# Seven products of quarters in a feed-forward input projection, with its features passed through DRAM

## The chip, the cores and the metric

The kernel runs on one core of one Trainium2 chip. A core has five engines that run side by side, each in its own order: TensorE (PE in the profile, with its weight loads shown apart as PEld), VectorE (DVE), ScalarE (ACT), GpSimd (POOL), and SyncE (SP), which here issues all transfers between DRAM and SBUF. Matrix products are summed in PSUM, which has eight banks of 512 fp32 numbers per partition. The metric is the device time of one execution in microseconds (us).

## The reference

Two layers of a decoder trunk, all in fp32, on 1024 prompt tokens and 8 sequences of 8 new tokens (1088 token columns in all). Layer 0 mixes tokens with an RG-LRU, layer 1 with HGRN2; after each mixer comes a feed-forward block, and each of the four sublayers ends in a residual sum and a layer norm:

```python
def causal_dwconv(x, buf, w, b):
    xp = jnp.concatenate([buf.astype(x.dtype), x], axis=1)
    y = sum(xp[:, j:j + L] * w[j] for j in range(width)) + b
    return y, xp[:, xp.shape[1] - (width - 1):]

def conv_ffn(x, buf, w_in, cw, cb, w_out):      # w_in 1024 x 5632, w_out 2816 x 1024
    gate, up = jnp.split(x @ w_in, 2, axis=-1)
    gc, new_buf = causal_dwconv(gate, buf, cw, cb)
    return (jax.nn.gelu(gc) * up) @ w_out, new_buf

for i in range(DEPTH):
    ...
    x = layer_norm(ALPHA * x + mix, ln_g[i, 0], ln_b[i, 0])
    f, fbuf = conv_ffn(x, ffn_conv[i], ffn_w_in[i], ffn_conv_w[i], ffn_conv_b[i], ffn_w_out[i])
    x = layer_norm(ALPHA * x + f, ln_g[i, 1], ln_b[i, 1])
```

## The kernel before

**Products.** TensorE multiplies in fp32r. Every fp32 operand is held as two fp32r parts, a high part `h` (the operand cast) and a low part `l` (operand minus `h`), and a product `a b` is made of three: `ah bh + ah bl + al bh`. Activations lie as features by tokens in `x[P, KT, 2, U]` (8 blocks of 128 features, two parts, 1088 tokens).

**Weights.** `stepf` writes down a list of steps, each with blocks of weights that it needs. `issue_raw` (L106) has SP load the next blocks into two staging tiles `raw`; `convert` (L115) splits a staged block of 128x1024 numbers: ACT casts it into the high part (L131) and the engine in `run["lo"]`, POOL from early on, subtracts (L132). Split blocks live in three tiles `wb` and in extra ones (`wx...`) where a stage has room. `pump` (L139) is called between groups of products and splits one block ahead. `fill` and `flush` take small closures from `pend`, which puts other work between the products.

**Feed-forward** (`ffn`, L781). The 2816 features are 22 blocks of 128. For each block `f` the gate product and the up product are made by `inproj` (L217): three chunks of 384, 384 and 320 tokens, each 8 feature blocks x 3 matmuls into one PSUM bank (`in_chunk`, L204). `g_evac` copies a gate out with ACT; `conv` (L829) makes the causal convolution with three DVE operations over 1104 columns, then GELU on ACT; `u_evac` (L844) multiplies by the up product and splits the result into the two parts of a tile `yf` in SBUF. After every two blocks `out_group` makes their share of the output product: 9 tiles of tokens (128 each, the last with the 64 new tokens) by 2 halves of 512 columns, 6 matmuls each, added to the residual in `z` by DVE (`resid`, L254). The last four blocks go in `out_final` with the layer norm.

**Layer norm** (`ln_pipeline`, L305) runs behind the last products of each tile of tokens: statistics on ACT and DVE, `nrm_b` scales on DVE (L281) and multiplies by the gain on POOL (L283), `nrm_c` adds the bias on DVE (L294). `to_x` (L237) then turns the tile into features with 8 transposes on TensorE, 2 ACT copies and 2 DVE subtractions. The last three tiles are left as fills for the next stage, which starts with `inproj_first` (L225), chunks of 512, 256 and 320 tokens. The sum before the first norm of a layer is made in `mix_out` (L434), in two passes of 9 tiles, one per half of the columns. `z` stays in SBUF between the two norms of a layer.

Of the kernel before, what the change touches and what calls it, by code (L numbers as in the profile page):

```python
# [18 lines left out]
P = 128  # L19
D = 1024  # L20
# [20 lines left out]
CH_FIRST = ((0, 512), (512, 256), (768, 320))  # L41
TW = 1152
# [14 lines left out]
def hawk_hgrn2_convffn_deepnorm_kernel(  # L57
# [15 lines left out]
    x = cp.tile([P, KT, 2, U], FR, name="x")  # L73
# [11 lines left out]
    zsave = dpool.tile([NT * P, D], F32, name="zsave")  # L85
    raws = [cp.tile([P, 1024], F32, name=f"raw{i}", tag=f"raw{i}") for i in range(2)]
# [5 lines left out]
    # ---------------------------------------------------------------- weight stream  # L92
# [4 lines left out]
    wfree = {"b": deque(wbase), "x": deque()}  # L97

    def stepf(phase, descr, fn, pref=None, keep=False):
        ids = []  # L100
        for i, b in enumerate(descr):
            blocks.append([phase, b, None, None, pref[i] if pref else "b"])
            ids.append(len(blocks) - 1)
        steps.append((phase, ids, fn, keep))

    def issue_raw(n=2):  # L106
        while run["dma"] < min(len(blocks), run["cvt"] + n) and rawq:
            b = blocks[run["dma"]]
            raw = rawq.popleft()
            dst, src = b[1](raw)  # L110
            sp.dma_start(dst, src)
            b[2] = raw
            run["dma"] += 1

    def convert():  # L115
        """Splits the next block of weights into its two parts, if a place for it is free."""
# [3 lines left out]
        kind = b[4]  # L120
        here = b[0] == run["phase"]
# [4 lines left out]
        b[4] = kind  # L126
        w = wfree[kind].popleft()
        issue_raw()
        raw = b[2]
        n = b[1].cols  # L130
        act.copy(w[:, 0, :n], raw[:, :n])  # L131
        run["lo"].tensor_tensor(w[:, 1, :n], raw[:, :n], w[:, 0, :n], ALU.subtract)  # L132
        b[3] = w
# [30 lines left out]
    def release(ids):  # L164
        for i in list(ids):
            b = blocks[i]
            if b[4] == "b" or b[0] == run["phase"]:
                wfree[b[4]].append(b[3])
            run["held"].remove(i)

    def run_steps(upto):
        while run["n"] < upto:
# [3 lines left out]
            while ids and run["cvt"] <= ids[-1]:  # L176
                assert convert(), "no place for weights"
            fn([blocks[i][3] for i in ids])
            held = run.setdefault("held", [])
            held.extend(ids)  # L180
            if not (keep and steps[run["n"] + 1][3]):
                release(held)
# [4 lines left out]
    # ---------------------------------------------------------------- helpers  # L187
# [36 lines left out]

    def inproj_first(ws, evacs):  # L225
        """The first products of a part: the last tiles of tokens are still on their way into x."""
# [10 lines left out]
    def to_x(m, src, rows):  # L237
        """Turns tokens into features: src [rows, 1024] -> x[:, :, :, tokens of tile m]."""
# [14 lines left out]
    # ---- residual and layer norm, one tile of tokens at a time  # L253
# [31 lines left out]
    def parts(m):  # L285
        """Who does what of a tile; nothing is left to hide the last one behind, and so it is shared."""
# [18 lines left out]
    def ln_pipeline(step_m, junks, final=None, between={}):  # L305
        """step_m(m, mid): the last products of tile m and their sums; the rest follows behind. It returns
        True if it has called mid itself, between its parts."""
        act.preload_act_table_set(LN_SET)
        order = [NT - 1] + list(range(NT - 1))
        run["end"] = order[-1] if final == "out" else None  # L310
        for i in range(NT + 2):
# [4 lines left out]
            if i < NT:  # L316
# [3 lines left out]
                nrm_a(order[i], junks[i % len(junks)])  # L320
# [9 lines left out]
            if final != "out" and 3 <= i < NT:  # L330
                m = order[i - 3]
                to_x(m, z[:, m], rows_of(m))
            run["bank"] = "s"
        if final != "out":
            for m in order[NT - 3:]:
                pend.append(lambda m=m: to_x(m, z[:, m], P))

    # ---------------------------------------------------------------- start
# [35 lines left out]
    def params_r():  # L374
# [24 lines left out]
        # Softmax over the layers of one kind (one of them here), its running sum less the first.  # L399
# [17 lines left out]
    # ---------------------------------------------------------------- output projection of a mixer  # L417
    def y_split(m, ks=range(0, KT)):
        if m < NT - 1:
            tk = slice(m * P, (m + 1) * P)  # L420
            k = slice(ks[0], ks[-1] + 1)
            act.copy(x[:, k, 0, tk], y8[:, k, tk])
            dve.tensor_tensor(x[:, k, 1, tk], y8[:, k, tk], x[:, k, 0, tk], ALU.subtract)
        else:
            tk = slice(SEQ, U)
            k = slice(ks[0], ks[-1] + 1)
            act.copy(ys[:, k, 0], y8[:, k, tk])
            dve.tensor_tensor(ys[:, k, 1], y8[:, k, tk], ys[:, k, 0], ALU.subtract)
# [5 lines left out]
    def mix_out(phase, w, z_src, li, stat_final, early=None):  # L434
        """early: (fills, close): the products of the first tiles with all but the last heads go first,
        with the fills between them."""
        banks = {}

        def prod_part(ps, m, ks, ws):
            if m < NT - 1:  # L440
                tk = slice(m * P, (m + 1) * P)
                for k in ks:
# [3 lines left out]
                    pe.matmul(ps, lhsT=x[:, k, 0, tk], rhs=wh, start=(k == 0), stop=False)  # L446
                    pe.matmul(ps, lhsT=x[:, k, 0, tk], rhs=wl, start=False, stop=False)  # L447
                    pe.matmul(ps, lhsT=x[:, k, 1, tk], rhs=wh, start=False, stop=(k == KT - 1))  # L448
# [21 lines left out]
        def pass0_early(ws):  # L470
            """The products with all but the last heads, and between them what is left of the mixer."""
# [1034 lines left out]
```

## Time and profile before

| | |
|---|---|
| median of 3 runs (lowest to highest) | 2661.74 us (2661.02 to 2662.32) |
| span of the profiled execution | 2662.3 us |
| that execution's own time | its span and under 1 us around it, as the runs lie at 2661.0 to 2662.3 |
| mean granted TensorE clock | 0.985 of full speed |
| read from HBM, written | 126.19 MB, 14.18 MB |
| feed-forward part of layer 0 and of layer 1 | about 343 to 1138 us, and 1865 to 2657 us |

The page gives busy time of each engine over the span, then the span in 40 slices, the transfers, the chain of work that ended last, and the costliest groups of instructions by line of the kernel. Matmul durations in it overlap one another, so the price of a matmul is taken from the distance between two starts. An instruction's row shows its duration with any time that it was held up after it had begun.

### The profile page before, as it was taken

How to read it: one execution, taken by the hardware profiler on the slowest of the kernel's cores; microseconds unless marked ns; L12 is line 12 of the kernel's file. 1: busy time of each engine (PE TensorE's matmuls, PEld its weight loads, DVE VectorE, ACT ScalarE, POOL GpSimd, SP SyncE). 2: the span in 40 equal slices, each digit the busy share in tenths (PEclk: the TensorE clock that was granted, in tenths of full speed). 3: DMA queues.
4: the chain of work that ended last, by engine and by line, in shares of the span. 5: the costliest groups of instructions: out<-in, count | busy, mean ns of one | idle time of the engine just before them, and what ended most of it. 6: DMA issues, size and time to landing. Idle time of an engine off the chain costs nothing. (4 is left out here: it accounts for less than half of the span.)

```text
span 2662.3 us, 35871 instructions
## 1 busy us (share of the span) xinstructions
PE 2607.3 (98%) x14951; PEld 2426.4 (91%) x14951; DVE 1489.8 (56%) x2240; ACT 857.1 (32%) x1419; POOL 955.5 (36%) x733
## 2 busy tenths in 40 slices
PE   9999999999999999999999999999999999999997
PEld 8999899999999999899988988878999999999996
DVE  5986454444444443758768484975444444444437
ACT  4775231121221212444444352443321221112223
POOL 2443342222222222436445463625422222222224
PEclk9999999999999999999899998999999999999999
DMA  4114111111111111221111111131211111111111
GB/s 130 38 44 157 32 56 48 44 44 48 44 45 48 40 48 38 81 64 57 41 32 41 49 41 49 42 105 51 72 40 48 45 43 48 40 48 48 40 40 70
DMA packets 181879, 142.67 MB, mean 54 GB/s; under 512 B 4881, under 2 KB 159633, under 8 KB 181678
## 3 DMA queue, kind: packets, MB, share of 16 engines
q1 hardware_dynamic: 181718, 140.39, 17.0%
q8 instruction: 117, 1.92, 0.3%
q14 instruction: 44, 0.36, 0.0%
HBM read 126.19 MB, written 14.18 MB: 53 GB/s over the span
## 5 line engine op out<-in xcount | busy, mean ns | idle before, releaser
L212 PE MATMUL ps_in<-x,wb 128*128 128x384 f32 (+2 forms) x2592 | 856.3, 330 | 0.2 <-ACT x L247 0.2
L213 PE MATMUL ps_in<-x,wb 128*128 128x384 f32 (+2 forms) x2592 | 849.3, 328 | 5.0 <-DVE x L248 5.0
L214 PE MATMUL ps_in<-x,wb 128*128 128x384 f32 (+2 forms) x2592 | 848.3, 327 | 0.0
L132 POOL TENSOR_TENSOR wb<-raw,wb 128x1024 fp32r<-128x1024 f32 (+1 forms) x156 | 380.6, 2440 | 1064.0 <-ACT wb L131 1039.0
L213 PEld LDWEIGHTS ps_in<-x,wb 128*128 128x128 f32 x2592 | 489.2, 189 | 8.4 <-DVE x L248 6.0
L212 PEld LDWEIGHTS ps_in<-x,wb 128*128 128x128 f32 x2592 | 488.9, 189 | 4.5 <-ACT x L247 0.5
L214 PEld LDWEIGHTS ps_in<-x,wb 128*128 128x128 f32 x2592 | 488.9, 189 | 2.1
L258 DVE SCALAR_TENSOR_TENSOR z<-z,ps_fo 128x512 f32<-128x512 f32 x320 | 220.1, 688 | 283.3 <-PE ps_fo L881 282.6
L131 ACT CAST wb<-raw 128x1024 fp32r<-128x1024 f32 (+1 forms) x159 | 161.9, 1018 | 289.8 <-issue 183.9
L860 DVE TENSOR_TENSOR tf<-tf,ps_in 128x384 f32<-128x384 f32 (+1 forms) x102 | 51.8, 508 | 283.5 <-PE ps_in L214 283.5
L879 PE MATMUL ps_fo<-wb,yf 128*128 128x512 f32 x448 | 174.8, 390 | 0.0
L881 PE MATMUL ps_fo<-wb,yf 128*128 128x512 f32 x448 | 174.7, 390 | 0.0
L880 PE MATMUL ps_fo<-wb,yf 128*128 128x512 f32 x448 | 174.4, 389 | 0.0
L132 POOL TENSOR_TENSOR wxf<-raw,wxf 128x1024 fp32r<-128x1024 f32 x32 | 76.8, 2401 | 240.0 <-ACT wxf L131 240.0
L212 PE MATMUL ps_in<-x,wxf 128*128 128x384 f32 (+1 forms) x480 | 156.5, 326 | 0.0
L213 PE MATMUL ps_in<-x,wxf 128*128 128x384 f32 (+1 forms) x480 | 156.4, 326 | 0.0
L214 PE MATMUL ps_in<-x,wxf 128*128 128x384 f32 (+1 forms) x480 | 156.4, 326 | 0.0
L283 POOL TENSOR_TENSOR z<-z,gb 128x1024 f32<-128x1024 f32 (+2 forms) x36 | 102.3, 2841 | 115.5 <-DVE z L281 115.5
L861 ACT CAST yf<-tf 128x384 fp32r<-128x384 f32 (+1 forms) x102 | 48.7, 477 | 257.0 <-DVE tf L860 257.0
L1101 POOL TENSOR_TENSOR z<-z 128x256 f32<-128x256 f32 x156 | 106.8, 716 | 61.4 <-DVE z L1074 23.3
L836 DVE SCALAR_TENSOR_TENSOR tf<-tf,ptf,tf 128x1104 f32<-128x1104 f32 x52 | 119.6, 2300 | 1.8
L881 PEld LDWEIGHTS ps_fo<-wb,yf 128*128 128x128 f32 x448 | 84.1, 188 | 18.0
(440 smaller groups left out, 4590.7 us busy)
## 6 DMA issues: line engine op xcount, KB each, us to landing
raw<-in_ffn_w_in_dram SPq DMA_DIRECT2D x88, 512.0 KB
raw<-in_ffn_w_out_dram SPq DMA_DIRECT2D x44, 512.0 KB
raw<-in_hg_w_in_dram SPq DMA_DIRECT2D x32, 512.0 KB
z<-in_x_prompt_dram SPq DMA_DIRECT2D x16, 512.0 KB
raw<-in_rg_w_in_dram SPq DMA_DIRECT2D x16, 512.0 KB
out_dram<-z SPq DMA_DIRECT2D x12, 512.0 KB
raw<-in_rg_w_out_dram SPq DMA_DIRECT2D x8, 512.0 KB
zsave<-z SPq DMA_DIRECT2D x8, 512.0 KB
```

What stands on the lines that cost most here:

```text
L131: act.copy(w[:, 0, :n], raw[:, :n])
L132: run["lo"].tensor_tensor(w[:, 1, :n], raw[:, :n], w[:, 0, :n], ALU.subtract)
L212: pe.matmul(ps[:, :n], lhsT=wh, rhs=xh, start=(k == 0), stop=False)
L213: pe.matmul(ps[:, :n], lhsT=wh, rhs=xl, start=False, stop=False)
L214: pe.matmul(ps[:, :n], lhsT=wl, rhs=xh, start=False, stop=(k == KT - 1))
L258: dve.scalar_tensor_tensor(zz, zz, a, ps, ALU.mult, ALU.add, accum_out=stat[:, m, n:n + 1] if acc else None)
L283: eng.tensor_tensor(z[:r, m, c], z[:r, m, c], gb[:r, 0, c], ALU.mult)
L836: dve.scalar_tensor_tensor(c[:, :L], gs[:, i:i + L], w[:, i:i + 1], c[:, :L], ALU.mult, ALU.add)
L879: pe.matmul(ps, lhsT=yh, rhs=wh, start=a, stop=False)
L880: pe.matmul(ps, lhsT=yh, rhs=wl, start=False, stop=False)
L881: pe.matmul(ps, lhsT=yl, rhs=wh, start=False, stop=b)
L1101: eng.tensor_tensor(ev[i], a, b, ALU.subtract)
```

## The change

**Input products by quarters.** In the feed-forward part the products of two feature blocks with all tokens are taken together, as a 2x2 by 2x2 product of quarters: weights by halves of the 1024 input features (two rows of quarters, 512 each) and by the two feature blocks (columns, 128 each), tokens by two halves of 544 (512 prompt tokens and 32 new ones). `products` makes seven products instead of eight, in Winograd's form: four sums of weight quarters, four sums of token quarters, seven sums of results. Each product is two chunks of 288 and 256 columns, 4 feature blocks x 3 matmuls each. Sums 5 to 7 go on in a PSUM bank that already holds an earlier product.

**Weights.** A pair of blocks is loaded into two staging tiles (four in all during the feed-forward part), and `convert_part` turns it into seven halves of a tile; each half takes an ACT copy of 128x512 and a POOL subtraction, four of them a POOL sum before. Eight halves are there; one is freed per product.

**Tokens.** `to_sums` replaces `to_x` ahead of a feed-forward part. It takes two tiles of tokens, one from each half, with 16 transposes, and makes seven operands: 8 ACT copies, 7 DVE operations, 4 POOL subtractions. It uses `z` as scratch, so `nrm_c` now saves `z` to DRAM (`zsave`) after the mixers too. The operands lie in the memory of `x` and in three tiles more. The tiles go through the layer norm in the order 8, 0, 4, 1, 5, 2, 6, 3, 7.

**Order.** All eleven pairs of gates and ups come first. The finished feature blocks are stored to DRAM in fp32 (`y_mul`, two transfers each), and loaded again into the memory that the operands leave (`y_load`), where `y_part` splits them. `turn` loads `z` from `zsave`. Then come the output products in groups of 6, 6, 6 and 4 feature blocks, so that one PSUM bank takes 18 matmuls instead of 6 before it is added to `z`.

**Ends of the mixers.** The last gate product is made with the features outermost (`inproj_last`) and the splits behind it are placed otherwise.

```diff
+    def convert_part(b):
+        issue_raw()
+        if len(b.raws) < 2:
+            return False
+        item = get_half(b.phase == run["phase"])
+        if item is None:
+            return False
+        (a11, a12), (a21, a22) = ((r[:, :512], r[:, 512:]) for r in b.raws)
+        i = len(b.w)
+        if i == 1:
+            pool.tensor_tensor(a21, a11, a21, ALU.subtract)
+        elif i == 2:
+            pool.tensor_tensor(a21, a22, a21, ALU.subtract)
+        elif i == 3:
+            pool.tensor_tensor(a11, a21, a11, ALU.add)
+        elif i == 6:
+            pool.tensor_tensor(a12, a12, a21, ALU.subtract)
+        src = (a11, a21, a21, a11, a12, a22, a12)[i]
+        w = item[0][:, :, item[1] * 512:(item[1] + 1) * 512]
+        act.copy(w[:, 0], src)
+        run["lo"].tensor_tensor(w[:, 1], src, w[:, 0], ALU.subtract)
...
+    def to_sums(mp):
...
+        def put(c, src, eng):
+            hi, lo = (xc[c][:, :, h, t0:t0 + n] for h in range(2))
+            act.copy(hi, src)
+            eng.tensor_tensor(lo, src, hi, ALU.subtract)
+
+        act.copy(t1, b12)
+        dve.tensor_tensor(t3, b22, t1, ALU.subtract)
+        dve.tensor_tensor(t1, t1, b11, ALU.subtract)
+        put(0, b11, dve)
+        dve.tensor_tensor(t2, b22, t1, ALU.subtract)
+        put(1, t3, pool)
+        put(2, t2, pool)
+        dve.tensor_tensor(t4, b21, t2, ALU.subtract)
+        put(3, t1, pool)
+        put(4, b21, dve)
+        put(5, t4, pool)
+        put(6, b22, dve)
...
+    BANK = ("A", "E", "B", "D", "A", "E", "D")
+    GROUPS = ((0, 6, 0), (6, 6, 6), (12, 6, 0), (18, 4, 8))
...
+        def products(b, places, first=False, fills={}):
...
+            def mm(i, c):
+                while len(b.w) <= i:
+                    assert convert(), "no place for weights"
+                w = b.w[i][0]
+                ps = bank(c, i)
+                c0, n = HCH[c]
+                for kk in range(4):
+                    wh, wl = (w[:, h, kk * P:(kk + 1) * P] for h in range(2))
+                    xh, xl = (xc[i][:, kk, h, c0:c0 + n] for h in range(2))
+                    for l, r in ((wh, xh), (wh, xl), (wl, xh)):
+                        pe.matmul(ps[:, :n], lhsT=l, rhs=r, start=(kk == 0 and i < 4 and l is wh and r is xh),
+                                  stop=(kk == 3 and l is wl), skip_group_check=(i >= 4))
...
+                if i == 0:
+                    for d, pv in q21:
+                        act.copy(d, pv(bk["A"]))
+                elif i == 2:
+                    add(q12, q21, bk["B"])
+                    add(q22, q12, bk["E"])
+                elif i == 3:
+                    add(q22, q22, bk["D"])
+                elif i == 4:
+                    for d, pv in q11:
+                        act.copy(d, pv(bk["A"]))
+                elif i == 5:
+                    add(q21, q12, bk["E"])
+                elif i == 6:
+                    add(q12, q12, bk["D"])
...
+            order = [(i, c) for c in range(2) for i in range(7)] if first else [(i, c) for i in range(7) for c in range(2)]
+            for i, c in order:
+                mm(i, c)
+                evac(i, c)
+                if c == 1:
+                    if i:
+                        put_half(b.w[i - 1][1])
+                    if i == 6:
+                        put_half(b.w[6][1])
+                if first or c == 1:
+                    pump()
+                for fn in fills.get((i, c), ()):
+                    fn()
...
+        def y_load(f, i):
+            sp.dma_start(yv[i][:, U:].bitcast(F32), ysave[f * P:(f + 1) * P])
+
+        def y_part(f, i):
+            y = yv[i]
+            for hi, lo in ((y[:, :SEQ], y[:, U + NS:]), (y[:, SEQ:U], y[:, U:U + NS])):
+                act.copy(hi, lo.bitcast(F32))
+                dve.tensor_tensor(lo, lo.bitcast(F32), hi, ALU.subtract)
...
+                if p:
+                    fills = {(0, 1): [lambda: y_mul(f0 - 2)], (1, 1): [lambda: y_mul(f1 - 2)]}
+                else:
+                    fills = {(2, 0): [fill], (4, 0): [flush]}
+                products(b, (g_place(f0), g_place(f1)), not p, fills)
...
+                cv = conv(f0) + conv(f1)
+                fills = {(i, c): [cv[2 * i + c]] for i in range(4) for c in range(2)}
...
+        def turn(_):
...
+            load_z(lambda m: zsave[m * P:m * P + rows_of(m)])
             load_gb(li, 1)
+            pend.extend([lambda i=i: y_part(i, i) for i in range(6, 12)])
```

More of the change, by code (lines that the diff above doesn't have):

```diff
@@ L119, in convert @@
         b = blocks[run["cvt"]]
-        kind = b[4]
-        here = b[0] == run["phase"]
+        if len(b.loads) == 2:
+            return convert_part(b)
+        kind = b.kind
+        here = b.phase == run["phase"]
         if kind == "a":
@@ L175, in run_steps @@
                 issue_raw()
[L176 to L182, printed above, removed]
+            pair = ids and len(blocks[ids[0]].loads) == 2
+            if pair:
+                fn(blocks[ids[0]])
+            else:
+                while ids and run["cvt"] <= ids[-1]:
+                    assert convert(), "no place for weights"
+                fn([blocks[i].w[0] for i in ids])
+                held = run.setdefault("held", [])
+                held.extend(ids)
+                if not (keep and steps[run["n"] + 1][3]):
+                    release(held)
             if ids:
@@ L223, in inproj, with inproj_last @@
                 fill(nfill)
+    def inproj_last(ws, ev, mids):
+        (w,) = ws
+        banks = [psi.tile([P, 512], F32, name="ps_in", tag="in") for _ in range(3)]
+        for k in range(KT):
+            wh = w[:, 0, k * P:(k + 1) * P]
+            wl = w[:, 1, k * P:(k + 1) * P]
+            for c, ps in enumerate(banks):
+                t0, n = run["ch"][c]
+                xh = x[:, k, 0, t0:t0 + n]
+                xl = x[:, k, 1, t0:t0 + n]
+                pe.matmul(ps[:, :n], lhsT=wh, rhs=xh, start=(k == 0), stop=False)
+                pe.matmul(ps[:, :n], lhsT=wh, rhs=xl, start=False, stop=False)
+                pe.matmul(ps[:, :n], lhsT=wl, rhs=xh, start=False, stop=(k == KT - 1))
+            if k in (2, 5):
+                pump()
+                mids()
+        for c, ps in enumerate(banks):
+            ev(c, ps)
+        pump()
+        mids()
     def inproj_first(ws, evacs):
@@ L303, in load_gb, with ln_pipeline, turn @@
         sp.dma_start(gb[:, 1], ln_b[i, j].partition_broadcast(P))
[L305 removed]
+    def ln_pipeline(step_m, junk, final=None, between={}, sums=False):
         act.preload_act_table_set(LN_SET)
[L309 removed]
+        order = [NT - 1] + ([0, 4, 1, 5, 2, 6, 3, 7] if sums else list(range(NT - 1)))
         run["end"] = order[-1] if final == "out" else None
+        def turn(m):
+            if not sums:
+                to_x(m, z[:, m], rows_of(m))
+            elif m >= 4:
+                to_sums(m - 4)
         for i in range(NT + 2):
@@ L769, in hawk_hgrn2_convffn_deepnorm_kernel, with gt_last @@
     stepf(0, [], lambda ws: (flush(), load_z(x_src)))
-    gt_step(7)
+    def gt_last(ws):
+        pend.extend([lambda: None, lambda: [y_split(m, range(7)) for m in range(4)]])
+        inproj_last(ws, gt_evac(7), fill)
+    stepf(0, [in_blk(W1, 7 * P)], gt_last)
     def rg_close(_):
```

466 lines of the change are left out of this document (291 added, 175 removed).

## The prediction, made before the changed kernel was run

> **What bounds the kernel now.** First the page: busy time by engine.
>
> ```profile
> span 2662.3 us, 35871 instructions
> PE 2607.3 (98%) x14951; PEld 2426.4 (91%) x14951; DVE 1489.8 (56%) x2240; ACT 857.1 (32%) x1419; POOL 955.5 (36%) x733
> ```
>
> TensorE is busy for 98%, every other engine for at most 56%. A share over the span hides stages, so next the table by stretches, for one turn of the feed-forward loop: the gates and ups of two feature blocks. Its columns are the stretch, its length, then busy us (and instructions) of PE, PEld, DVE, ACT and POOL, the granted clock, the DMA share and GB/s.
>
> ```profile
> 442.26:489.63 47.37, 47.37 (x289) 47.36 (x288) 19.27 (x24) 11.49 (x20) 14.96 (x12) 1.00 0.15 45
> ```
>
> 288 matmuls fill 47.37 us without a gap, at full clock, with POOL busy for 15 us and DVE for 19. There are 11 such turns a layer, 22 in all: 1042 us, bound by the stream of matmuls alone. What TensorE saves there comes off the time, as long as no other engine needs longer for the same turn.
>
> **The change part by part.**
>
> *Matmuls.* A turn had 4 products x 8 feature blocks x 3 matmuls x 3 chunks = 288, on 384, 384 and 320 columns. It becomes 2 x 7 products x 4 x 3 x 2 chunks = 336, on 288 and 256 columns: 7/8 of the columns, a sixth more instructions. The price is the distance between starts, from the timeline of TensorE; here the first and last of 22 matmuls on 256 columns, of 18 on 320, and of 15 output matmuls on 512, with DVE's addition of their results below:
>
> ```profile
> 357.80 0.28 PE L214 MATMUL ps_in<-x,wb 128*128 128x256 f32 x1
> ...
> 360.27 0.28 PE L214 MATMUL ps_in<-x,wb 128*128 128x256 f32 x1
> 700.11 0.31 PE L212 MATMUL ps_in<-x,wb 128*128 128x320 f32 x1
> ...
> 702.60 0.31 PE L214 MATMUL ps_in<-x,wb 128*128 128x320 f32 x1
> 702.75 0.40 PE L879 MATMUL ps_fo<-wb,yf 128*128 128x512 f32 x1
> ...
> 705.97 0.39 PE L881 MATMUL ps_fo<-wb,yf 128*128 128x512 f32 x1
> L258 DVE SCALAR_TENSOR_TENSOR z<-z,ps_fo 128x512 f32<-128x512 f32 x320 | 220.1, 688 | 283.3 <-PE ps_fo L881 282.6
> ```
>
> 2.47 us over 21 steps is 0.118 us for 256 columns, 2.49 over 17 is 0.1465 for 320; 288 lies halfway, 0.132. A turn takes 168 x 0.132 + 168 x 0.118 = 22.2 + 19.8 = **42.0 us**, 5.4 less, and 22 turns save **118 us**. Ends: by columns alone 41.4 us (131 saved); with 288 columns as dear as 320, 168 x 0.1465 + 19.8 = 44.4 (65 saved). I take the line between the rows, as each shape there was measured with a weight load per matmul.
>
> The output products keep their 104 matmuls per two blocks. Their longer groups only spare DVE additions (0.69 us each), which lie beside 6 matmuls of 0.23 (3.22 us over 14 steps): nothing.
>
> *Splitting of weights.* This moves the most work, to POOL. Rows with x/y/z give minimum/median/maximum in ns, rows with bars the sum in us and the mean in ns, rows that begin with a time its start and us:
>
> ```profile
> L132 POOL TENSOR_TENSOR wb<-raw,wb x156: 741/2408/4802, 18.6 to 2579.8; 128x1024 fp32r<-128x1024 f32 x148, 128x256 fp32r<-128x256 f32 x8
> L247 ACT CAST x<-ps_t 128x512 fp32r<-128x512 f32 x64 | 34.0, 588 | 4.9 <-PE ps_t L245 4.7
> 501.49 1.05 ACT L131 CAST wb<-raw 128x1024 fp32r<-128x1024 f32 x1 [10.22 <-issue]
> 502.62 2.40 POOL L132 TENSOR_TENSOR wb<-raw,wb 128x1024 fp32r<-128x1024 f32 x1 [8.87 <-ACT wb L131]
> L834 DVE TENSOR_SCALAR tf<-tf,ptf 128x1104 f32<-128x1104 f32 x26 | 22.1, 850 | 0.0
> L294 DVE TENSOR_TENSOR z<-z,gb x34: 1206/1292/3405, 307.5 to 2657.4; 128x1024 f32<-128x1024 f32 x30, 64x1024 f32<-64x1024 f32 x3, 128x768 f32<-128x768 f32 x1
> L855 DVE TENSOR_TENSOR tf<-tf,ps_in 128x64 f32<-128x64 f32 x34 | 7.5, 222 | 62.0 <-PE ps_in L214 62.0
> L836 DVE SCALAR_TENSOR_TENSOR tf<-tf,ptf,tf x20: 1367/2376/3391, 457.1 to 981.6; 128x1104 f32<-128x1104 f32 x20
> 551.77 3.39 DVE L836 SCALAR_TENSOR_TENSOR tf<-tf,ptf,tf 128x1104 f32<-128x1104 f32 x1
> 551.54 2.46 POOL L132 TENSOR_TENSOR wb<-raw,wb 128x1024 fp32r<-128x1024 f32 x1 [10.48 <-ACT wb L131]
> 553.94 1.27 POOL L838 COPY fs<-tf 128x2 f32<-128x2 f32 x1
> 555.15 0.19 POOL L840 COPY fs<-tf 128x16 f32<-128x16 f32 x1
> ```
>
> POOL takes 0.74 us for 128x256 (the minimum) and 2.41 for 128x1024, so about 1.30 for 128x512. A turn needs 2 x (7 subtractions + 4 sums) = 22 of these, 28.6 us, and small copies for 1.4: 30 where it had 15. Eight times the order is sum on POOL, copy on ACT (0.6 us, and 0.15 for two hand-overs, as 501.49 + 1.05 to 502.62 is 0.08), subtraction on POOL, so POOL also waits 8 x 0.75 = 6: **36 us** of 42.
>
> Then line 836 and the rows below it. Alone, DVE's step of the convolution takes 1.37 us; begun beside a POOL subtraction it took 3.39, as it stood until that one ended. POOL's copy of 128x2 then took 1.27 behind DVE, and the copy after it, alone, 0.19. A DVE operation on two SBUF operands and a POOL operation take turns. A turn has such DVE work: per feature block 0.85 + 2 x 1.37 for the convolution and about 1.43 for `y_mul` (1.21 for 128x1024 at the least, 0.22 for the 64 columns), 5.0, so **10.1 us** for two. If it all falls into POOL's waits and idle time, POOL needs 36 us a turn; if none does, 46.1. I take 42.7: a third of it hidden, as POOL stands idle for a sixth of its chain and DVE's pieces come in bunches. That is 0.7 over TensorE's 42.0, **16 us** in 22 turns; ends 0 and 4.1 x 22 = 90. ACT stands in line behind POOL's sums, and its copy of a result must be out of bank A before the fifth product adds to it, 12 us into a turn of 21, so a lag of POOL is forgiven up to some 10 us only.
>
> *Start of a feed-forward part.* Before, its seam looks so:
>
> ```profile
> 342.08 0.40 PE L448 MATMUL ps_o<-wx0a,x 128*128 128x512 f32 x1
> 350.16 3.32 POOL L283 TENSOR_TENSOR z<-z,gb 128x1024 f32<-128x1024 f32 x1 [1.85 <-DVE z L281]
> 353.44 2.39 POOL L132 TENSOR_TENSOR wb<-raw,wb 128x1024 fp32r<-128x1024 f32 x1
> 357.57 0.39 PE L213 MATMUL ps_in<-x,wb 128*128 128x256 f32 x1 [1.32 <-DVE x L248]
> ```
>
> The mixer's last matmul starts at 342.1, POOL's last gain ends 11 us later, and TensorE loses 1.3 us, as both blocks of weights were ready or next. After, only two of seven halves can be split ahead (one free tile; the others hold the mixer's weights until its last matmul). The third needs POOL behind its last gain: at about 11 us, sum, copy, subtraction, and DVE's bias in between, so 15 us, where TensorE has done its first two products by 3. The rest comes at POOL's pace: halves four to seven at 18, 19, then, behind four subtractions for tokens (`to_sums`, 5.2 us), 26 and 30. The first seven products on 288 columns end near 31 instead of 11 + 2 for transposes. The other seven find their weights ready and run 10 us. So TensorE stands for 18 us, 16 net of what such a seam lost before: **32 us** for two layers. Ends: 8 a layer, if POOL's gain ends earlier than before; 25, if `to_sums` holds up the last tiles.
>
> The Trainium skill speaks against this place: TensorE: Matmul & The Clock Gate, section The HAM clock gate, says that an idle window of about 3.4 us halves the array's clock. Here the row 1690:1760 (further down) agrees in kind; by that rule the start would cost some 2 us a layer more, and the sum would be 4 higher.
>
> *Features through DRAM, and the turn to the output.* Stores lie beside the loop. At the turn, 12 loads of 557 KB follow the products as their memory comes free.
>
> ```profile
> 246.00:248.00 2.00, 2.00 (x10) 1.64 (x9) 1.80 (x2) 2.00 (x4) 0.00 (x0) 1.00 1.07 399
> 1690.00:1760.00 70.00, 63.72 (x351) 53.66 (x350) 62.44 (x102) 33.23 (x51) 33.37 (x35) 0.90 0.13 39
> ```
>
> In the first row the DMA engines are full at 399 GB/s, so a load takes 1.4 us; the first six, issued 3 to 9 us into the last ups of 21, are in by 14. Their splits (ACT 1.05 and a tail, DVE 1.43 us each) end with those products. `z` is loaded behind the last store, about 12 us later, while four PSUM banks take 4 x 18 x 0.23 = 17 us of products. I take 2 us, and 2 more for the third and fourth block of the last group's weights, split only when a tile comes free: **8 us** for two layers. Ends: 0, and 28 a layer if the 12 loads (17 us) and then `z` (4.5 MB, 11 us) stand open.
>
> *Mixers' ends.* `to_sums` has 7 DVE operations (0.68 each from PSUM) for two tiles instead of 4, and `nrm_c` 5 more saves on SP. They lie beside 11 us of matmuls for two tiles; their delay is in the start above. `inproj_last` moves splits whose readers come 5 us later: nothing.
>
> Sum, from the profiled execution (span 2662.3; with what lies around it, within 1 us of the median 2661.74): 2662.3 - 118 + 16 + 32 + 8 = **2600 us**.
>
> **The rivals.**
>
> *A: POOL takes TensorE's place, and the kernel gets slower.* POOL's chain of sums, copies and subtractions, with DVE's turns in it, sets the turn. For it: the rows of lines 836 and 838. Against it: 36 us without DVE, and POOL idle in gaps that DVE can use. At 46.1 us a turn the gain of 118 shrinks by 90: 2662 - 28 + 32 + 8 = 2674. It decides from a turn of 45.5 us on: there 3.5 x 22 = 78 and the 40 at the seams eat the 118. The Trainium skill states this as a rule: SBUF — State Buffer, section Who interferes with whom, has the port pair of the two engines as an exclusive lock for a whole instruction. The rows of lines 836 and 838 agree with it (3.39 for 1.37 us).
>
> *B: all is covered.* POOL keeps under 42 us, and the seams cost half: 2662 - 118 + 16 + 4 = 2564. For it: 36 us of POOL, DVE free for half of the turn. Against it: the start's chain, read off POOL's own rows.
>
> *C: the turn stands open.* The loads and `z` come one behind another with no products beside them, 28 us a layer: 2662 - 118 + 16 + 32 + 56 = 2648. Against it: 399 GB/s and a block of 21 us to load in.
>
> *D: the change does not save what it says,* as 336 weight loads cost as much as 320 columns: 336 x 0.1465 = 49.2 us a turn, 40 more in all, 2758 with the seams. The 256-column rows, with a weight load each, speak against it.
>
> **How the numbers follow.** Forecast 0.50 (2580 to 2630 by its own ends), A 0.18, B 0.19, C 0.11, D 0.02. The predicted time is the forecast's, 2600. The range runs from 2560, just past B, to 2670, which takes in C and the milder part of A; above it lie D and A at its worst, below it the column-only price with all covered. A measurement of this kernel tells about 0.2% (5 us) from no change. Faster by more: the forecast, B, C, and of A what stays under a turn of 45 us (0.02): 0.82. Within: 0.05 of A, near its point of decision. Slower: 0.11 of A, and D: 0.13.
>
> **What would show it.** In the changed kernel's table by stretches, two blocks of gates and ups should take 42 to 43 us with 336 matmuls, and POOL be busy for 30 us and more of it, its instructions longer than 1.30 where DVE runs. Starts 0.118 apart on 256 columns and 0.132 on 288 show the matmul term; a turn near 46 with matmuls waiting for DVE or ACT is A. At the start, the gap between the mixer's last matmul and the third product, ended by POOL's subtraction, should be about 10 us, and the clock below 1.00 near it. At the turn, a gap above 5 us ended by a load or by a split is C. The forecast is wrong if a matmul's price goes with its number rather than its columns, or if POOL's and DVE's turns cost more than the one operation each that the rows show.

## The result, and the profile after

The changed kernel takes 2646.45 us (median of 4 runs, 2643.24 to 2650.27) beside 2661.38 for the kernel before: a ratio of 0.9943, 95% interval 0.9929 to 0.9957. It is faster, by 15 us where 61 were forecast. The profiled execution took 2643.24 us.

The page's head: busy time by engine over the span.

```profile
span 2641.5 us, 39929 instructions
PE 2528.3 (96%) x16007; PEld 2332.4 (88%) x16007; DVE 1566.3 (59%) x2412; ACT 950.4 (36%) x1643; POOL 1425.1 (54%) x1169
```

POOL has gone from 36% to 54%. The table by stretches shows the feed-forward loop in bulk: 420 us of each layer's gates and ups, then two windows of 42.08 us, early and late in layer 0 (columns as in the prediction).

```profile
400.00:820.00 420.00, 420.00 (x3340) 419.82 (x3339) 242.66 (x350) 132.78 (x262) 344.86 (x304) 1.00 0.26 78
1910.00:2330.00 420.00, 419.87 (x3339) 419.66 (x3338) 242.96 (x351) 133.20 (x263) 343.80 (x303) 1.00 0.26 78
442.08:484.16 42.08, 42.08 (x337) 42.08 (x337) 25.03 (x36) 12.53 (x26) 35.61 (x32) 1.00 0.25 77
694.56:736.64 42.08, 42.08 (x337) 42.08 (x336) 23.69 (x35) 13.54 (x26) 33.80 (x31) 1.00 0.26 77
```

In these windows of layer 0 TensorE has no gap, at full clock. The last two are a little shorter than a turn: from the first gate product of one pair to that of the next, TensorE's timeline has 42.25 us (42.22 to 42.30 from the third pair on), where it had 47.37. The products save nearly what they should. The saving is lost at the seams. The next rows are what TensorE waited for, first at the start of layer 0's feed-forward part (340 to 400 us; waits in all, times, longest), then at the seam into HGRN2 (1120 to 1165):

```profile
PE ps_f L1045 <- ACT wb L185: 12.9, 1, 12.9
PE ps_t L373 <- DVE x L391: 2.4, 2, 1.9
PE ps_f L1045 <- POOL wxf L186: 0.8, 1, 0.8
...
PE ps_in L300 <- POOL wb L215: 6.1, 1, 6.1
PE ps_in L298 <- ACT wb L214: 5.4, 1, 5.4
```

The timeline of TensorE and DVE at the turn to the output (the first output product starts at 839.46), and of the stretches of the start and of the turn:

```profile
835.96 7.58 DVE L1131 TENSOR_TENSOR xa<-xa 128x1024 fp32r<-128x1024 f32 x8 [1.80 <-ACT xa L1130]
843.46 0.77 DVE L1050 TENSOR_TENSOR z<-z,ps_f 128x288 f32<-128x288 f32 x2
844.15 6.94 DVE L1131 TENSOR_TENSOR xa<-xa 128x1024 fp32r<-128x1024 f32 x4
847.57 0.79 PE L1146 MATMUL ps_fo<-wxf,xa 128*128 128x512 f32 x1 [3.56 <-DVE xa L1131]
851.01 0.80 PE L1146 MATMUL ps_fo<-wxf,xa 128*128 128x512 f32 x1 [1.80 <-DVE xa L1131]
860.51 0.69 DVE L411 SCALAR_TENSOR_TENSOR z<-z,ps_fo 128x512 f32<-128x512 f32 x1 [6.06 <-DMA z<-zsave]
```
```profile
345.40:376.60 31.20, 14.89 (x93) 13.59 (x93) 18.95 (x34) 11.63 (x24) 24.17 (x20) 0.78 0.27 84
376.60:400.00 23.40, 21.41 (x146) 20.29 (x145) 10.49 (x18) 9.16 (x19) 18.79 (x16) 0.85 0.17 47
842.20:851.00 8.80, 2.59 (x6) 1.02 (x5) 8.80 (x7) 8.80 (x15) 6.91 (x3) 0.71 0.32 126
851.00:856.20 5.20, 5.18 (x12) 4.13 (x13) 3.42 (x7) 0.50 (x2) 0.00 (x0) 0.50 0.45 175
```

TensorE stood until DVE had split blocks 4 and 5, and at the start and here the clock fell to half during or behind the stand. One more loss lies in the output products behind the turn. The next two rows show TensorE's output products alone (busy us, count, clock, DMA share, GB/s), first in the kernel before, then in the changed one, where the count has one that had begun earlier:

```profile
702.75:726.50 23.75, 23.75 (x104) 1.00 0.13 44
870.02:1038.95 168.93, 168.93 (x729) 1.00 0.25 90
```

Without a wait and at full clock, their starts lie 0.232 us apart (168.93 over 728) where they lay 0.228. That is some 4 us in the 976 of a layer; no run shows why. Put together from the distances between starts in TensorE's timeline, for both layers:

| part | forecast | measured | how |
|---|---|---|---|
| products | -118 | -112.6 | 22 x (47.37 - 42.25) |
| POOL as the bound | +16 | 0 | no wait of TensorE in 400:840 |
| starts | +32 | +48.4 | first product to first output product 494.1 and 494.0 us, 11 turns are 464.8: 29.3 a layer; before, a turn and a half (71.1) took 76.2: 5.1 |
| turn and output products | +8 | +28.2 | 976 matmuls in 237.9 and 237.7 us; before 223.7 (nine groups of 23.62 or 23.76, 213.3 in all, and 40 matmuls in 10.40) |
| seam into HGRN2 | 0 | +10.1 | last output matmul to the first of `v`: 41.1 for 31.0 us |
| mixers' ends and the rest | 0 | +5.0 | 4.6 and 1.9 longer, after 1.5 less ahead of them |
| sum | -62 | -20.9 | the spans differ by 20.8 |

### The profile page after: what moved, and what is told of

Its sections match the earlier page's. It is cut to its first block, busy times and chain, and to the rows that moved or that the text cites. A ratio compares the mean times of both kernels' runs of the same rounds, so it can differ in the third digit from the quotient of the medians.

```text
span 2641.5 us, 39929 instructions
## 1 busy us (share of the span) xinstructions
PE 2528.3 (96%) x16007; PEld 2332.4 (88%) x16007; DVE 1566.3 (59%) x2412; ACT 950.4 (36%) x1643; POOL 1425.1 (54%) x1169
## 5 line engine op out<-in xcount | busy, mean ns | idle before, releaser
L215 POOL TENSOR_TENSOR wb<-raw,wb 128x1024 fp32r<-128x1024 f32 (+1 forms) x80 | 195.8, 2451 | 577.2 <-ACT wb L214 371.6
L1045 PE MATMUL ps_f<-xa,wb 128*128 128x288 f32 (+1 forms) x3072 | 406.9, 293 | 28.4 <-ACT wb L185 24.3
L1045 PEld LDWEIGHTS ps_f<-xa,wb 128*128 128x128 f32 x3072 | 398.9, 192 | 32.0 <-ACT wb L185 24.9
L1050 DVE TENSOR_TENSOR z<-z,ps_f 128x256 f32<-128x256 f32 (+2 forms) x550 | 196.2, 378 | 364.8 <-PE ps_f L1045 307.9
L1045 PE MATMUL ps_f<-x,wb 128*128 128x288 f32 (+1 forms) x2496 | 322.8, 289 | 0.0
L1045 PEld LDWEIGHTS ps_f<-x,wb 128*128 128x128 f32 x2496 | 318.1, 189 | 0.0
L298 PE MATMUL ps_in<-xa,wb 128*128 128x384 f32 (+3 forms) x912 | 307.4, 337 | 5.7 <-ACT wb L214 5.4
L300 PE MATMUL ps_in<-xa,wb 128*128 128x384 f32 (+3 forms) x912 | 300.5, 330 | 6.1 <-POOL wb L215 6.1
L299 PE MATMUL ps_in<-xa,wb 128*128 128x384 f32 (+3 forms) x912 | 300.6, 330 | 0.3 <-DVE xa L356 0.3
L186 POOL TENSOR_TENSOR wb<-rawf,wb 128x512 fp32r<-128x512 f32 x116 | 165.6, 1436 | 57.0 <-ACT wb L185 56.3
L1098 DVE SCALAR_TENSOR_TENSOR z<-z,ptf 128x1104 f32<-128x1104 f32 x88 | 182.0, 2069 | 1.6
L298 PEld LDWEIGHTS ps_in<-xa,wb 128*128 128x128 f32 x912 | 173.7, 190 | 8.4 <-ACT wb L214 5.7
L300 PEld LDWEIGHTS ps_in<-xa,wb 128*128 128x128 f32 x912 | 173.2, 190 | 7.5 <-POOL wb L215 6.8
L299 PEld LDWEIGHTS ps_in<-xa,wb 128*128 128x128 f32 x912 | 173.7, 190 | 1.4 <-DVE xa L356 0.7
```

The costliest lines, as they stand in the source:

```text
L186: run["lo"].tensor_tensor(w[:, 1], src, w[:, 0], ALU.subtract)
L298: pe.matmul(ps[:, :n], lhsT=wh, rhs=xh, start=(k == 0), stop=False)
L299: pe.matmul(ps[:, :n], lhsT=wh, rhs=xl, start=False, stop=False)
L300: pe.matmul(ps[:, :n], lhsT=wl, rhs=xh, start=False, stop=(k == KT - 1))
L1045: pe.matmul(ps[:, :n], lhsT=l, rhs=r, start=(kk == 0 and i < 4 and l is wh and r is xh), stop=(kk == 3 and l is wl), skip_group_check=(i > ...
L1050: dve.tensor_tensor(d, s, pv(ps), ALU.add)
```

## The experiments

All are edits of the changed kernel. Ratios are against the kernel before, with a 95% interval; the changed kernel's own is 0.9943, so 0.001 is 2.7 us. Of the seams each trace tells more sharply than the time: the stretch up to the first gate product took 345.4 to 348.1 us even in kernels whose edits all lie behind it.

**The gain of the last two tiles on DVE.** At the start, POOL's queue held the gains of tiles 3 and 7 (3.4 and 3.3 us) ahead of the third weight half.

```diff
     def parts(m):
...
+        if m in run.get("gdve", ()):
+            return (dve, slice(0, D)),
         return (pool, slice(0, D)),
...
+        run["gdve"] = order[-2:] if sums else ()
```


> Theory: the start of a feed-forward part is set by POOL's queue. The third half of weights stands behind POOL's gains of the last two tiles (3.4 us each, until 360.3), and TensorE waits 13.2 us for it. With these two gains on DVE (1.2 us each) POOL is free from 351 on, the third product begins some 7 us earlier, and the kernel gains 2 x 7 = 14 us over the changed kernel (2646 to about 2632). Rival: the token operands or DVE are late next; then the gap becomes shorter, but the second set of products waits for it, and the gain is under 5 us.

2637.2 us, 0.9907 (0.9892 to 0.9922). The wait for the third half fell from 12.9 to 7.6 us, but first product to first output product only from 494.1 to 490.0 (490.2 in layer 1). POOL's queue is part of the cause; something else takes over. Two rows of ACT's timeline, then TensorE's waits in this kernel's loop (395 to 830 us), show both:

```profile
355.87 1.15 ACT L422 ACTIVATE junk<-z,stat 128x1024 f32<-128x1024 f32 x1 [5.34 <-DVE stat L421]
...
357.58 0.60 ACT L185 CAST wb<-raw 128x512 fp32r<-128x512 f32 x1
```
```profile
PE ps_f L1048 <- ACT z L1068: 1.3, 1, 1.3
PE ps_f L1048 <- ACT z L1060: 0.5, 1, 0.5
```

The copy of the half now stands behind the square sum of the last norm, and in the loop, where there was no wait before, TensorE waits 1.8 us for ACT's copies of finished banks, which stand in line behind POOL's sums: POOL has not caught up with the earlier start.

**Two halves ahead of the last norm.** Added to the edit above:

```diff
                 pump()
+                if i == NT - 1 and sums:
+                    for j in steps[run["n"]][1]:
+                        if blocks[j].kind == "b":
+                            wfree["b"].append(blocks[j].w[0])
+                            blocks[j].kind = "gone"
+                    for _ in range(2):
+                        convert()
                 nrm_a(order[i], junk())
```


> As e1_gain_dve, and halves three and four of the weights are put in line before the last tile's norm, as soon as their memory is free. Theory: in e1_gain_dve the third product still waited 7.6 us, for ACT's copy of the third half, which stood behind the last tile's square sum (ACT's row of 355.87) though its sum was ready at 353.6; ahead of it the third product begins 4 to 5 us earlier, so 8 to 10 us less than e1_gain_dve (2637), about 2628. Rival: the second set of seven products waits for the last tokens, whose norm and split end no earlier; then the time moves from the third product to there and the gain is under 4 us.

2645.3 us, 0.9933 (0.9918 to 0.9948): worse than without. The wait at the third product fell to 3.6 us, and the time moved to the last tokens, as the rival had it, but more of it. What TensorE waited for at this start, and the row of ACT behind it:

```profile
PE ps_t L373 <- ACT z L393: 10.8, 1, 10.8
PE ps_f L1056 <- ACT wb L185: 3.6, 1, 3.6
```
```profile
374.21 0.62 ACT L185 CAST wxf<-rawf 128x512 fp32r<-128x512 f32 x1 [5.53 <-DMA rawf<-in_ffn_w_in_dram]
```

With the first pair's halves done early, the next pair's came up, and ACT stood in line for their transfer while the last tokens waited behind it.

**Matmuls by zero in the gaps.** Weights of zero, added to banks that are being summed, so that the array is busy where it stood.

```diff
+                if first and (i, c) == (2, 0):
+                    for _ in range(85):
+                        pe.matmul(banks[0, "E"][:, :256], lhsT=zero, rhs=xc[1][:, 0, 0, 0:256], start=False, stop=True, skip_group_check=True)
...
                     pe.matmul(ps, lhsT=yh, rhs=wl, start=False, stop=False)
+                    if (f0, m, n) == (0, 0, 0) and j >= 4:
+                        for _ in range(14 if j == 4 else 6):
+                            pe.matmul(ps, lhsT=zero, rhs=wh, start=False, stop=False)
                     pe.matmul(ps, lhsT=yl, rhs=wh, start=False, stop=b)
```


> TensorE multiplies by zeros in the gaps: 85 matmuls of 256 columns (10 us) in the start's gap of 13.2 us, 14 and 6 of 512 columns in the turn's gaps of 3.8 and 2.2 us, and 44 transposes and 24 matmuls in the seam into HGRN2. The waits for data stay as they are. Theory: beside its wait each gap costs a stretch at half clock (13.7 us at the start, 10.2 at the turn, 10.2 at HGRN2); counted by the matmuls begun in them, 21 x 0.125, 15 x 0.23 and 9 x 0.23 us are lost there. So the 0.50 stretches behind the filled gaps vanish and the kernel gains 2 x (2.6 + 3.5) + 2 = 14 us (about 2632). Rival: the pace there is that of the supply, and full clock only makes the waits longer: under 4 us, with the clock at 1.00 all the same.

2641.2 us, 0.9921 (0.9907 to 0.9936): 5 us less by the medians, near the rival, though this interval and the changed kernel's (0.9929 to 0.9957) overlap. Stretches of the start and of the turn in this kernel, then TensorE's waits in the loop behind (403 to 840 us):

```profile
348.10:379.40 31.30, 25.16 (x174) 23.90 (x173) 18.71 (x33) 11.74 (x24) 23.75 (x20) 0.89 0.27 84
379.40:403.00 23.60, 21.12 (x162) 20.03 (x163) 10.45 (x21) 9.17 (x19) 19.01 (x15) 1.00 0.17 45
...
845.60:854.40 8.80, 6.53 (x26) 4.35 (x24) 8.80 (x7) 8.80 (x15) 6.99 (x3) 1.00 0.32 120
```
```profile
PE ps_f L1054 <- ACT z L1074: 1.4, 1, 1.4
PE ps_f L1054 <- ACT z L1066: 0.6, 1, 0.6
```

The clock is 1.00 where it was 0.85 and 0.71. The turn gained 2.1 us a layer (237.9 to 235.8) and HGRN2's seam 1.2, also some 5 in all; here full clock was worth something only where the work behind the gap wasn't itself short of supply. What it won at the start (174 + 162 - 85 matmuls by 403 for 93 + 146 by 400, some 1 us) came back as 2.0 us of waits in the loop: 494.7 and 493.7 us, nothing gained. Over the whole span 21 us of clock were won (1 - 0.972 of 2641.5 us, 1 - 0.980 of 2640.4), and some 5 of time.

**Blocks 4 and 5 in a second sweep.** The first four output tiles keep their banks open.

```diff
+                        early = {}
+                        if n == 0 and gi == 0:
+                            for m in range(4):
+                                early[m] = sbank("ps_fo")
+                                part(early[m], m, grp, ws, range(4))
                         for m in range(NT):
-                            prod(m, n, grp, ws, gi == 0, False)
+                            if m in early:
+                                part(early[m], m, grp, ws, range(4, 6))
+                                resid(m, n, early[m], True, False)
+                            else:
+                                prod(m, n, grp, ws, gi == 0, False)
```


> The first four output tiles take feature blocks 0 to 3 first and blocks 4 and 5 in a second sweep; same matmuls. Theory: the turn costs 13.7 us a layer, because DVE splits blocks 4 and 5 until 851 and TensorE, which asks for them 2.8 us after it starts, waits 7.1 us and then runs at half clock for 10.2 us. With 11 us of other matmuls ahead the gaps and the half clock go: 2 x 11 = 22 us less than the changed kernel (about 2624). Rival: the loads of z and the additions behind them are late next, at four banks full; then the gap moves to some 12 to 17 us after the start, and the gain is under 8 us.

2638.2 us, 0.991 (0.9896 to 0.9925). The 976 matmuls took 233.6 us in both layers (237.9): the waits for splits went, but one of another kind came, for DVE's addition that frees a bank, at 849 (838 to 880 us):

```profile
PE ps_fo L1148 <- DVE z L1050: 3.9, 1, 3.9
```

**And the additions first.** `y_mul` and the last products' additions ahead of the splits of 4 and 5:

```diff
                     for i in range(3, 6):
...
-                        fills[i, 1].extend([lambda i=i, j=j: y_part(2 * i + j - 6, 2 * i + j - 6) for j in range(2)])
+                        if i < 5:
+                            fills[i, 1].extend([lambda i=i, j=j: y_part(2 * i + j - 6, 2 * i + j - 6) for j in range(2)])
...
                     y_mul(f0)
                     y_mul(f1)
+                    y_part(4, 4)
+                    y_part(5, 5)
```


> As e2_turn_split, and DVE takes the last products' additions and y_mul before it splits blocks 4 and 5. Theory: in e2_turn_split the wait of 3.9 us was for a PSUM bank, whose addition stood on DVE behind the splits of blocks 4 and 5; with the additions first it goes, z is loaded some 6 us earlier, and the turn's 13.7 us (9.4 in e2_turn_split) fall to 2 to 4: about 2626. Rival: the splits, begun after y_mul at about 849 and done at 853, are late for the second sweep, which begins 11 us after the first product; then 2 us of wait and a stretch at half clock stay, and the gain over e2_turn_split is under 6 us.

2627.4 us, 0.9865 (0.9851 to 0.988). 229.3 us in both layers, 8.6 less than the changed kernel. The stretch of the turn, and its two waits:

```profile
842.70:851.50 8.80, 8.80 (x39) 7.10 (x39) 8.77 (x10) 8.80 (x16) 7.07 (x3) 1.00 0.74 287
```
```profile
PE ps_fo L1150 <- DVE xa L1131: 0.8, 2, 0.5
```

39 matmuls where there were 6, with DVE and ACT as busy as before: the turn was an order of DVE's queue, not a lack of engine time or of bandwidth.

**HGRN2's first block ahead.** The last output group, four blocks of weights, took all three common tiles and one of the two extra ones, so none was left that HGRN2 may use.

```diff
+        if kind == "c":
+            kind = "x" if here and wfree["x"] else "b"
...
-                stepf(phase, [out_blk(WO, f0, 0), out_blk(WO, f0, 1), out_blk(WO, f0 + 2, 0), out_blk(WO, f0 + 2, 1)], fn, "aaaa")
+                stepf(phase, [out_blk(WO, f0, 0), out_blk(WO, f0, 1), out_blk(WO, f0 + 2, 0), out_blk(WO, f0 + 2, 1)], fn, "cccc")
```


> The last output group takes the two extra weight tiles first, so one of the three common tiles is free for HGRN2's first block of weights before the group ends. Theory: the seam into HGRN2 loses 10 us since its two first blocks are split only behind the last group (waits of 5.4 us for ACT and 6.1 us for POOL, then half clock); with one block split ahead, as in the kernel before, both waits and the half clock go: 10 us less than the changed kernel (about 2636). Rival: POOL's gains (until 1134) hold the second block anyway, and the wait moves there: under 4 us.

2639.3 us, 0.9913 (0.9896 to 0.9929). In TensorE's waits there (1115 to 1165 us) the one for ACT is gone and the other stands; the seam is 4.9 us shorter.

```profile
PE ps_in L302 <- POOL wb L217: 6.1, 1, 6.1
```

**And the second block ahead of the last norm**, by the edit of e6_halves_ahead, at this place and for one block.

> As e3_hg_ahead, and HGRN2's second block of weights is put in line before the last tile's norm. Theory: e3_hg_ahead took one of the two waits away (5.7 us) and kept the other, 6.5 us for POOL's subtraction of the second block behind the gains of the last two tiles; ahead of the last gain it ends at about 1130 instead of 1137, so 4 to 6 us less than e3_hg_ahead (2639), about 2634. Rival: POOL is held by the gain of the last tile but one until 1127 and ACT by the same norm; under 2 us.

2636.05 us, 0.9899 (0.9885 to 0.9914). Of the waits in the same stretch one is left, for the tokens of the last tile:

```profile
PE ps_in L301 <- DVE xa L358: 2.7, 1, 2.7
```

The seam takes 4.4 us less than in e3_hg_ahead, 9.3 less than in the changed kernel: nearly all of the loss is made good.

**POOL's slack.** One subtraction of seven made twice in layer 0, two in layer 1:

```diff
         run["lo"].tensor_tensor(w[:, 1], src, w[:, 0], ALU.subtract)
+        if i in {1: (5,), 3: (2, 5)}[b.phase]:
+            pool.tensor_tensor(w[:, 1], src, w[:, 0], ALU.subtract)
```


> POOL makes one subtraction of seven twice in layer 0 (2 x 1.3 = 2.6 us a turn more) and two of seven in layer 1 (5.2 us). Theory: in the changed kernel POOL is busy 33.8 to 35.6 us of a turn of 42.08 and waits some 7 for ACT's copies, which it can't use, so its chain is 41 to 42 us and has next to no slack: turns of 43.5 and 46 us, the loop 10 to 15 us longer in layer 0 and 35 to 45 in layer 1. Rival: the 6.5 to 8 us in which POOL isn't busy are slack that the additional work fills: turns of 42.08 in both layers, no change of the loops' 494 us.

2711.3 us, 1.0179 (1.0162 to 1.0196). The loop with its start took 509.8 us in layer 0 and 540.4 in layer 1 (494.1 and 494.0). From the third pair on, a turn took 43.7 us in layer 0 and 46.5 in layer 1 on average, 1.5 and 4.2 more, close to the 43.5 and 46 of the theory. 420 us of each layer, and TensorE's waits in the second:

```profile
400.00:820.00 420.00, 406.01 (x3208) 403.77 (x3207) 241.59 (x333) 122.43 (x251) 356.50 (x306) 1.00 0.24 73
1960.00:2380.00 420.00, 393.84 (x3043) 390.75 (x3043) 225.05 (x316) 112.75 (x234) 358.67 (x308) 0.98 0.23 70
```
```profile
PE ps_f L1047 <- ACT z L1067: 23.0, 9, 2.8
PE ps_f L1047 <- ACT z L1059: 3.1, 4, 0.8
```

POOL is shown busy for 85% of these stretches and is nevertheless the bound. In the changed kernel the waits of POOL itself (400 to 820 us) say why:

```profile
POOL wb L186 <- ACT wb L185: 48.2, 63, 1.5
POOL wxf L186 <- ACT wxf L185: 19.6, 25, 1.4
POOL wb L186 <- PE ps_f L1045: 5.1, 7, 0.7
POOL wxf L186 <- PE ps_f L1045: 0.7, 1, 0.7
```

344.9 us busy and 67.8 in line for ACT's copies are 412.7 of 420; only 5.8 us, the waits for a half that TensorE has yet to give back, were slack: 0.6 us a turn. The two layers of e7_pool_twice give a little more: of 2.6 and 5.2 us of work added, 1.1 and 1.0 didn't show in the turn.

**Three repairs together**: the edits of e1_gain_dve, e5_turn_order and e8_hg_both.

> The edits of e1_gain_dve, e5_turn_order and e8_hg_both together. Theory: the seams are separate, so their gains over the changed kernel (2646) add: 9, 19 and 10 us by the medians, to about 2608. Rival: they share a resource, or the common shift of the loads brings a new wait; then over 2616.

2610.8 us, 0.9804 (0.9789 to 0.9818). The seams' times are those of the single runs: 490.1 and 490.2 us of products, 230.0 of output products in both layers, and the seam into HGRN2 9.4 us shorter. So they add, and the rival falls.

**One half ahead.** As the three, with one half before the last norm, and the next pair's halves held back:

```diff
-                if first or c == 1:
+                if first and not (c == 0 and i < 4 and b.ready) or c == 1:
                     pump()
```


> As c1_three, with one half of the weights (not two, as in e6_halves_ahead) put in line before the last tile's norm, and no half of the next pair before the last tokens are split. Theory: in e6_halves_ahead the gain at the third product was lost again because ACT stood in line for the transfer of the next pair (5.5 us until 374) ahead of the last tokens, and because two copies delayed the last norm by 3 us; without both, the third product begins 3 to 4 us earlier than in e1_gain_dve and the last tokens no later: 4 to 8 us less than c1_three, about 2602. Rival: the last tokens, split from 368 to 382 in e1_gain_dve, set the end of the start whatever the weights do: under 2 us.

2608.7 us, 0.98 (0.9784 to 0.9817): 489.2 us where the three had 490.1. The third product waits 3.7 us instead of 7.6, and the transposes of the last tokens have a new wait of 3.9: the rival.

**Another order in `to_sums`**, alone and with all others: ACT's three copies from PSUM directly behind its first, DVE's four sums ahead of its three subtractions.

> The changed kernel with another order inside to_sums: ACT copies first what it takes from PSUM, and DVE makes its four sums one after the other before its subtractions. Theory: DVE is in to_sums for 6.7 us a pair of tiles and idle for 3.2 of them in waits for ACT, which delays the norm behind it, on which the next transposes wait (2.7 us) and at the start the last tokens; with 2 us a pair less the mixers' ends lose 2 us less each and the start 2 to 4: 6 to 12 us less than the changed kernel, about 2637. Rival: the start hangs on the weight halves alone: only the 2 us at each mixer's end, under 5 in all.

> c2_one_half and e12_sums_order together. Theory: with the weights out of the way, the start hangs on the last tokens, so the shorter to_sums counts in full: 6 to 10 us less than c2_one_half. Rival: DVE's norm and gain set it, and it gives under 3.

Alone 2644.1 us, 0.9935 (0.992 to 0.9949), which can't be told from the changed kernel: 0.7 us less in the first mixer's output sums (104.6 for 105.3), 1.6 to 2.5 more from the first product to the first output product, where TensorE now waits 5.8 us for the subtractions that were put last. With all 2605.0 us, 0.9783 (0.9769 to 0.9798), 3.7 us less than c2_one_half with intervals that overlap, between theory and rival. First product to first output product took 488.2 and 489.7 us (489.2 and 489.3 in c2_one_half), so a gain at the starts isn't shown. It is the best version: 2.2% under the kernel before.

## Why the prediction was half right

Faster was right, and 2646 lies in the range of 2560 to 2670; a quarter of the forecast gain came. What failed is the price of the seams and of the output products: 40 us were put down for them, and they cost 92.

**Matmuls: right.** 42.0 us a turn forecast, 42.25 measured; 118 us forecast, 113 saved. Time goes with columns here, as the 256- and 320-column rows said, and rival D falls.

**Splitting of weights: right in its mechanism, mis-sized by 1.2 us a turn, 16 in all.** 42.7 us of POOL's chain were forecast; it is 41.5 (412.7 us in the 9.94 turns of those 420). Its parts: 34.7 busy for the 30 forecast, so some 4.7 of the 10.1 us of DVE's turns fall on POOL, and 6.8 in line for ACT (6 forecast). As 41.5 is under 42.25, nothing of it reaches the time. The point from which rival A decides was within reach: e7_pool_twice, with 2.6 and 5.2 us more, made turns of 43.7 and 46.5 and a kernel slower than before. TensorE waited where the prediction had it, behind ACT's copies of results.

The Trainium skill (SBUF — State Buffer, section Who interferes with whom) has a DVE operation with two SBUF operands and a POOL operation that reads SBUF shut each other out for a whole instruction. The traces agree, here in two rows of DVE's timeline at the start, where the second bias ran beside POOL's L178 of 360.25:

```profile
356.87 1.22 DVE L447 TENSOR_TENSOR z<-z,gb 128x1024 f32<-128x1024 f32 x1
360.32 2.27 DVE L447 TENSOR_TENSOR z<-z,gb 128x1024 f32<-128x1024 f32 x1 [2.23 <-POOL z L436]
```

**Start: a step that failed, by 16 us.** The stand was well forecast (18 us; the waits sum to 18.1), with a third product that waits 12.9 us where 10 were named, behind POOL's last gains as described. What failed is the step from there to the end of the first fourteen products: that the first seven end 31 us after the mixer's last matmul begins, and that the other seven find their weights ready and run 10. In TensorE's timeline the first seven ended at 36.8 and the others took 13.0. So the start cost 29.3 us a layer, where 18 and 3.2 of transposes would be 21. Half clock (the clock was 0.78 and 0.85 in the two stretches) explains the second number in part: at full clock, in e4_zeros, the other seven took 10.9, but the first seven ended no earlier (37.4), and the time won was lost again in the loop. The runs showed something more: the start has two chains of like length, halves and last tokens, and POOL's pace in the loop behind it. Taking 5 to 9 us off the wait for the third half gave 4 to 5 (e1_gain_dve, c2_one_half) or nothing (e6_halves_ahead). How the missing 8 us a layer divide between these isn't shown.

By the rule of the Trainium skill (TensorE: Matmul & The Clock Gate, section The HAM clock gate) the prediction named 2 us a layer for half clock, beside its sum. The stretches agree with the rule in kind, and are longer than thought (13.7 and 6.8 us at the start, 10.2 at the turn); the last section has one that came without so long a stand. e4_zeros shows that they cost little when taken away at the start.

**Turn and output products: the step that failed most, by 20 us.** That the splits end with the last products held for four blocks of six. DVE, full from 836 on, took the splits of 4 and 5 from 844 to 851, 6.9 us beside POOL's weights where e5_turn_order's row below has 2.6 without them, and TensorE had come to them at 842.2. TensorE waited for `z` in none of the runs; DVE did, beside products (6.06 us in the row of 860.51). Rival C had the right place and the wrong resource: no transfer stood open, DVE's order did, for some 10 us a layer and not 28, of which e5_turn_order gave 8.6 back. The other 4 of the 14.1 us a layer are the output matmuls, 0.232 us apart for 0.228. The prediction put them at nothing, and no run takes them away.

```profile
853.68 2.62 DVE L1131 TENSOR_TENSOR xa<-xa 128x1024 fp32r<-128x1024 f32 x4
```

**Seam into HGRN2: not in the sum, 10 us.** The prediction saw that the last group's weights need four tiles and priced their own lateness; it didn't ask what the next stage finds when they are taken. e8_hg_both gives 9.3 of the 10 us back.

**Mixers' ends: "nothing" was 5 us.** Transposes waited 2.7 us for the bias of a tile, whose norm stood on DVE behind the previous `to_sums`. That it is DVE's waits for ACT inside `to_sums` which do this was argued; e12_sums_order shortened the stage by 0.7 us only, so how the 4.6 us divide stays open.

So the products gave 113 us, and of the 92 that came back 33 (spans of 2641.5 and 2608.4 us) were repaired by three edits of order, which lands the kernel 11 us from the forecast. That is luck in part: POOL's 16 us, forecast and not paid, stand against losses that remain, some 40 us at the starts, 13 in the output products and 5 at the mixers' ends.

## What to carry to other kernels

When a change moves work from the bounding engine to another, add that engine's waits in line to its busy time before calling it free: POOL at 82% busy had some 1 us of slack in a turn of 42. And price each seam by walking the queues of all engines in their order, the next stage's first weights and buffers among them: a speed-up inside a loop is worth its seams, and at the turn here the order of a queue was worth more than the work in it.

## What the runs showed of the hardware that wasn't expected

In the changed kernel half clock came in stretches of 3.4, 6.8, 10.2 and 13.7 us (only the last, which ends with the program, has another length), late and whole. Stretches of the start, whose stand began at 349.3:

```profile
349.20:354.40 5.20, 0.08 (x1) 0.00 (x0) 4.47 (x12) 1.74 (x4) 3.87 (x3) 1.00 0.01 6
354.60:362.20 7.60, 0.00 (x0) 0.00 (x0) 5.26 (x6) 0.66 (x2) 5.58 (x3) 0.50 0.31 124
362.20:368.10 5.90, 5.18 (x21) 4.81 (x22) 1.36 (x5) 1.98 (x5) 5.14 (x8) 0.50 0.86 235
```

And of e4_zeros, where a stand of only 3 us sufficed:

```profile
362.10:365.10 3.00, 0.19 (x2) 0.00 (x0) 1.86 (x1) 0.65 (x2) 2.32 (x2) 1.00 0.33 134
365.40:372.00 6.60, 5.77 (x25) 5.40 (x25) 1.08 (x5) 1.69 (x4) 5.87 (x9) 0.50 0.89 241
```

Not even that was needed. In the changed kernel the clock came back at 368.2 and was halved again at 381.8, though no two matmuls in a row in between began more than 2.2 us apart:

```profile
378.40:381.80 3.40, 1.89 (x13) 1.61 (x12) 1.29 (x2) 1.98 (x5) 2.55 (x3) 0.99 0.06 14
381.80:388.60 6.80, 6.32 (x29) 5.67 (x28) 4.40 (x10) 4.01 (x8) 5.32 (x5) 0.50 0.54 151
```

So a long stand isn't the only thing that brings half clock. More than half of the first stretch of 13.7 us (354.5 to 362.2) fell on time in which the array stood anyway. Its price is therefore not half of its length: in e4_zeros 21 us less of lost clock were worth some 5 us.
